# Live rows as plus and minus one, a reordered start, and loop counters raised earlier: masked self-attention on one core

## The chip, the cores and the metric

One core of one Trainium2 chip runs the whole batch as one program. The metric is device microseconds of one execution, shown as the median of the runs. Five engines work side by side: TensorE (PE, with its weight loads as PEld), VectorE (DVE), ScalarE (ACT), GpSimd (POOL) and SyncE (SP), which issues most transfers. Each engine has its own list of instructions and its own sequencer, and the lists meet only at semaphores. The times are from one fixed draw of the lengths.

## The reference

```python
batch, max_seq, n_heads, head_dim = (32, 512, 8, 64)
lengths = np.random.randint(64, max_seq, size=batch)
...
for b in range(batch):
    seq_len = lengths[b]
    qkv = np.matmul(x[b, :seq_len], w_qkv)
    q, k, v = np.split(qkv, 3, axis=-1)
    ...
    scores = scale * np.matmul(q, k.transpose(0, 2, 1))
    attn = np.exp(scores - scores_max)
    attn = attn / (np.sum(attn, axis=-1, keepdims=True) + 1e-08)
    output[b, :seq_len] = np.matmul(attn, v)...
```

Rows at and behind `seq_len` stay zero in the output. Everything is float32 in and out; the kernel multiplies in float16 with float32 sums.

## The kernel before

**Order by length.** The kernel ranks the 32 sequences by length on the chip and works them off in 16 pairs, longest first. There are twelve loops, one for each padded width N in `LOOPS` (512, 448, 384, 352 and so on by 32 down to 96). A loop runs as often as there are pairs of its width; for this draw once for 512, 448, 384, 320, 288, 256, 192, 128 and 96, three times for 352, twice for 224 and 160. A loop's body holds two positions, one for each sequence of the pair. A width has n = 4, 3, 2 or 1 tiles of 128 rows.

**Steps.** What a position does and in which order is written by hand in the table `ORDER`: S is a step of scores with its exponentials, B, Q and K are query and key projections, U, V and W values, A and Z weighted sums, E fills columns, L writes the live column, P the masks and casts, D loads, X transposes by DMA. The digits after @ are the eight PSUM banks that a step uses (512 fp32 in a partition each). A position projects the sequence behind it while it computes the weighted sums of its own. So TensorE's next group waits for a bank until VectorE or ScalarE has copied it out.

**Normalisation.** The value matmuls carry a 65th column, so that a bank holds the weighted sums of some heads and beside them the sum of each row's exponentials. VectorE then runs, for each head group, R (reciprocal of the sums into `rcp`, L1706), U (times the live rows, 1 or 0, from the live column of `v_aug` or from `queries`, L1712) and O (the bank times the broadcast `rcp` into `out_nat`, L1715). For two neighbouring banks with n = 2, or one tile, `both_normed` does this over both at once (L1671, L1680, L1693). With n = 1 `divide_live` (L1725) multiplies by the live row and `rcp` in one scalar_tensor_tensor instead of U and O.

**Waits.** Semaphores are only counted up, so a wait inside a loop compares against a register. Every engine holds `pair` and one register for each distinct amount; at the end of a loop's body it adds to each of them, and on entering a loop it works out a few more by a multiply and an add (`fixed`). TensorE's additions are rows L2115 and L2123 in its list, its branch back L2125, its entry L2088 and the loop's first compare L2102. A wait that a planner (`plan_waits`) finds to be covered by an earlier one is left out.

**The head.** Ahead of the loops the first sequence is cast to 16 bits tile by tile (L366 on VectorE, L370 on ScalarE, L371 on GpSimd), transposed on TensorE (L773) and projected: v0 to v3 (L311), then queries and keys (L300), which start with the first two quarters of the weights. The casts of the weights (L750) are shared by ScalarE and GpSimd. GpSimd also fills the ends of the `et` buffers (L590, L601). `joinPE` is the point at which TensorE waits for ScalarE's last transposed copy (L782); then come the registers, the branch and the first scores (L1269).

## Time and profile before

| what | value |
|---|---|
| runs | 329.23, 328.48, 329.05 us; median 329.05 |
| profiled execution's own time | its span, 328.5 us from the first to the last instruction; granted TensorE clock 0.994 |
| PE, ACT, DVE, POOL busy | 311.6, 262.6, 197.7, 101.9 us |
| head, until the first scores | 22.7 us |
| loops 512; 448; 384; 352 (three times) | from 22.7; 59.3; 91; 116 |
| loops 320; 288; 256; 224 (twice) | from 189; 211; 232; 246 |
| loops 192; 160 (twice); 128; 96 | from 275; 288; 310; 317 |
| end of the last division, of the store | 323.2, 328.5 us |

In the rows of the profile a start is given in us from the span's start, then the duration in us, the engine, the line, the operation, the tile written and those read, shapes, the count of merged instructions, and in brackets how long the engine stood idle before and what ended that. "issue" is time in which the engine waited for nothing that the profile shows. Where rows are grouped, the last columns are busy us, mean ns of one, and idle us before them.

### The profile page before, as it was taken

How to read it: one execution, taken by the hardware profiler on the slowest of the kernel's cores; microseconds unless marked ns; L12 is line 12 of the kernel's file. 1: busy time of each engine (PE TensorE's matmuls, PEld its weight loads, DVE VectorE, ACT ScalarE, POOL GpSimd, SP SyncE). 2: the span in 40 equal slices, each digit the busy share in tenths (PEclk: the TensorE clock that was granted, in tenths of full speed). 3: DMA queues.
4: the chain of work that ended last, by engine and by line, in shares of the span. 5: the costliest groups of instructions: out<-in, count | busy, mean ns of one | idle time of the engine just before them, and what ended most of it. 6: DMA issues, size and time to landing. Idle time of an engine off the chain costs nothing.

```text
span 328.5 us, 13310 instructions
## 1 busy us (share of the span) xinstructions
PE 311.6 (95%) x5092; PEld 202.3 (62%) x5092; DVE 197.7 (60%) x635; ACT 262.6 (80%) x413; POOL 101.9 (31%) x148
## 2 busy tenths in 40 slices
PE   6899999999999999999999999999998999999980
PEld 4444645555655556556656657667777886777860
DVE  6777567566666646456455465545575565776853
ACT  4379999897878988988978989899867779687761
POOL 6448040324030330330231243043222224435320
PEclk9999999999999999999999999999999999999997
DMA  6984749395858999696676766857459857966651
GB/s 217 382 278 80 251 140 327 76 354 153 304 52 298 224 269 258 197 268 224 233 214 224 255 194 205 211 174 242 156 131 227 183 176 164 223 206 177 193 180 66
DMA packets 69449, 68.85 MB, mean 210 GB/s; under 512 B 40720, under 2 KB 40720, under 8 KB 69392
## 3 DMA queue, kind: packets, MB, share of 16 engines
q1 hardware_dynamic: 69344, 68.12, 71.4%
q8 instruction: 33, 0.54, 0.7%
q14 instruction: 24, 0.20, 0.2%
q10 hardware_dynamic: 48, 0.00, 0.0%
HBM read 25.17 MB, written 33.55 MB: 179 GB/s over the span
## 4 chain that ended last, share of the span: by engine, by line
PE 84%; DVE 5%; DMA 3%; issue 2%; ACT 2%; SPq 1%; POOL 1%; DVEq 0%; POOLq 0%; ACTq 0%
PE banks L1323 41%; PE banks L1269 13%; PE banks L1517 12%; PE banks L300 6%; PE banks L311 6%; PE banks L1631 2%; DMA xT<-x 2%; DMA x_nat<-in_x_dram 2%; PE banks L1210 1%; PE banks L1557 1%; DVE out_nat L1715 1%; DVE rcp L1712 1%; DVE out_nat L1693 1%; SPq L328 1%; ACT et L1287 1%
## 5 line engine op out<-in xcount | busy, mean ns | idle before, releaser
L1287 ACT ACTIVATE et<-banks 128x704 f16<-128x704 f32 (+8 forms) x256 | 198.8, 825 | 27.8 <-PE banks L1269 24.7
L371 POOL TENSOR_TENSOR x<-x_nat,mask 128x512 f16<-128x512 f32 x83 | 84.2, 1041 | 184.3 <-DVE mask L1052 174.9
L1323 PE MATMUL banks<-xT,w_r 64*128 64x352 f16 (+9 forms) x1536 | 127.8, 294 | 1.8 <-DMA xT<-x 1.2
L1323 PEld LDWEIGHTS banks<-xT,w_r 64*128 64x128 f16 x1536 | 68.7, 94 | 39.0 <-PE banks L1323 8.5
L1269 PE MATMUL banks<-qz,kT 64*128 64x352 f16 (+11 forms) x624 | 77.5, 294 | 2.6 <-issue 0.7
L1715 DVE TENSOR_TENSOR out_nat<-banks,rcp 128x256 f32<-128x256 f32 (+1 forms) x110 | 53.0, 482 | 3.8
L1367 DVE CAST qz<-banks 128x448 f16<-128x448 f32 (+6 forms) x47 | 26.4, 561 | 45.2 <-PE banks L1323 44.8
L1517 PEld LDWEIGHTS banks<-v_aug,et 128*128 128x128 f16 x1240 | 41.7, 97 | 13.5 <-issue 6.8
L1517 PE MATMUL banks<-v_aug,et 128*128 128x65 f16 x1240 | 47.1, 194 | 0.0
L1323 PE MATMUL banks<-w_r,xT 64*128 64x512 f16 (+1 forms) x368 | 46.6, 372 | 0.3 <-ACT v_aug L1489 0.3
L1269 PEld LDWEIGHTS banks<-qz,kT 64*128 64x128 f16 x624 | 28.1, 93 | 25.9 <-issue 7.1
L1706 DVE RECIPROCAL rcp<-banks 128x4 f32<-128x4 f32 (+1 forms) x112 | 20.3, 181 | 20.7 <-PE banks L1517 7.3
L311 PE MATMUL banks<-w_r,xT 128*128 128x512 f16 x104 | 26.9, 381 | 0.5 <-DVE xT L782 0.5
L1386 DVE CAST v_aug<-banks 128x512 f16<-128x512 f32 x25 | 16.6, 690 | 17.9 <-PE banks L1323 17.9
L1323 PEld LDWEIGHTS banks<-w_r,xT 64*128 64x128 f16 x368 | 17.2, 94 | 14.1 <-PE banks L1323 1.0
L1367 ACT CAST kT<-banks 128x352 f16<-128x352 f32 (+6 forms) x47 | 22.5, 479 | 1.5 <-PE banks L1323 1.5
L300 PE MATMUL banks<-xT,w_r 128*128 128x160 f16 (+3 forms) x256 | 23.0, 243 | 0.5 <-DVE v_aug L1489 0.5
L1367 DVE CAST kT<-banks 128x352 f16<-128x352 f32 (+5 forms) x33 | 17.9, 552 | 7.7 <-PE banks L1323 7.6
L300 PEld LDWEIGHTS banks<-xT,w_r 128*128 128x128 f16 x256 | 16.6, 98 | 5.2 <-DMA xT<-x 0.6
L1367 ACT CAST qz<-banks 128x352 f16<-128x352 f32 (+6 forms) x33 | 15.3, 465 | 3.7 <-PE banks L1323 3.6
L1489 ACT CAST v_aug<-banks 128x512 f16<-128x512 f32 x15 | 8.8, 589 | 9.5 <-PE banks L311 9.5
L1631 PE MATMUL banks<-v_aug,et 64*128 64x65 f16 x624 | 14.2, 190 | 0.6 <-issue 0.6
(116 smaller groups left out, 193.3 us busy)
## 6 DMA issues: line engine op xcount, KB each, us to landing
x_nat<-in_x_dram SPq DMA_DIRECT2D x12, 768.0 KB, 6.4
out_dram<-out_nat SPq DMA_DIRECT2D x12, 768.0 KB, 4.0
x_nat<-in_x_dram SPq DMA_DIRECT2D x14, 512.0 KB, 4.5
out_dram<-zeros SPq DMA_DIRECT2D x12, 512.0 KB, 3.6
out_dram<-out_nat SPq DMA_DIRECT2D x12, 512.0 KB, 4.7
out_dram<-out_nat SPq DMA_DIRECT2D x4, 1024.0 KB, 7.0
x_nat<-in_x_dram SPq DMA_DIRECT2D x3, 1024.0 KB, 5.3
out_dram<-zeros SPq DMA_DIRECT2D x4, 768.0 KB, 4.7
```

Of the source, the lines that this page charges most:

```text
L300: last = nc.tensor.matmul(dst[:, 0:N], w_r[:, c, w0 : w0 + P], xT[:, c, 0:N], start=(c == 0), stop=(c == NC - 1),)
L311: last = nc.tensor.matmul(pv, xT[:, c, t * P : (t + 1) * P], w_r[:, c, 2 * D : 3 * D], start=(c == 0), stop=(c == NC - 1),)
L371: return engine.tensor_tensor(out=x16, in0=x32, in1=live.broadcast_to([P, D]), op=ALU.mult)
L1269: last = nc.tensor.matmul(psc[par][:, x * wide : x * wide + N], kT[r, i, c0 : c0 + P], qz[r, i, 0:N], start=True, stop=True,)
L1287: return nc.scalar.activation(out=et[:, :, x0:x1, 0:N], in_=got.rearrange("p j (x q) -> p j x q", q=wide)[:, :, x0:x1, 0:N], func=AF.Exp, ...
L1323: last = nc.tensor.matmul(to, lhs(rows, c), rhs(rows, c), start=(c == 0 and opens), stop=(c == NC - 1 and not opens),)
L1367: return lambda copy, bank: copy(out=buf[:, ms, 0:M], in_=bank[:, 0 : gm * M].rearrange("p (m q) -> p m q", q=M),)
L1386: return lambda copy, bank: copy(out=v_bufs[o][:, t, :, 0:HD], in_=bank.rearrange("p (h d) -> p h d", d=HD))
L1517: last = nc.tensor.matmul(pav[:, g, qt, :], e_bufs[e][:, c0 + qt * P : c0 + (qt + 1) * P], v_aug[:, kt, h, :], start=(kt == 0 and not (hal ...
L1631: last = nc.tensor.matmul(pavs[own][:, g, qt, :], e_bufs[e][rows, c0 + qt * P : c0 + (qt + 1) * P], (v_bufs[0] if ending else v_aug)[rows, ...
L1706: return nc.vector.reciprocal(out=rcp, in_=pav[:, :, :, HD])
L1715: return nc.vector.tensor_tensor(out=o_t[:, 0:n, h0 * HD : (h0 + heads) * HD].rearrange("p t (g d) -> p g t d", d=HD), in0=pav[:, :, :, 0:HD],
```

## The change

1. **Live rows.** `queries` holds 2 x alive - 1, so +1 for a live row and -1 for one behind the end. For n > 1, U comes first and multiplies the sums in PSUM by it into `rcp`; R takes the reciprocal of `rcp` in SBUF; O becomes a scalar_tensor_tensor that takes the larger of `rcp` and 0 and multiplies the bank by it, so that dead rows come out as zeros. Its patterns need the sums of a bank in the order tile, head, column. A `both_normed` over two tiles becomes two such operations. The loops of 448, 320 and 192 no longer copy the live rows into `queries` on entry (L1851); a `queries` operation is added in the head and, in loops without a half last tile, at the second position's L.
2. **The head.** The fourth tile is cast by ScalarE, its transposes stand ahead of v2, some VectorE copies change places, GpSimd's fills come behind its weight casts, two banks of the key projections are exchanged, the last key copy goes to ScalarE, and TensorE works out its first registers ahead of `joinPE`.
3. **Counters.** In the loops of `LATE`, TensorE raises `pair` and its registers ahead of its last one to three operations of the second position; these then ask for amounts that are smaller by as much. Waits for another loop's position use one of three registers set by one move at a loop's entry.
4. **The last position.** In the second position of the loop of 96, A0 over banks 3 and 4 becomes two steps of four heads.

TensorE in the head, from the first transposes to the query projections; `x_73` is the first sequence in 16 bits, L311 the value projections. Before:

```order
L773 MATMUL banks<-h_ident_117,x_73 128x128 x4
L311 MATMUL banks<-w_r,xT_75 128x512 x4
L773 MATMUL banks<-h_ident_117,x_73 128x128 x4
L311 MATMUL banks<-w_r,xT_75 128x512 x8
L773 MATMUL banks<-h_ident_117,x_73 128x128 x4
L311 MATMUL banks<-w_r,xT_75 128x512 x4
```

and with the change:

```order
L754 MATMUL banks<-h_ident_117,x_73 128x128 x4
L314 MATMUL banks<-w_r,xT_75 128x512 x4
L754 MATMUL banks<-h_ident_117,x_73 128x128 x4
L314 MATMUL banks<-w_r,xT_75 128x512 x4
L754 MATMUL banks<-h_ident_117,x_73 128x128 x4
L314 MATMUL banks<-w_r,xT_75 128x512 x8
```

The last four transposes moved ahead of v2, so that eight value matmuls follow them.

TensorE at the end of the loop of 288 and the first scores of 256 (`qz`, `kT`); ISA and REGISTER_ALU are register operations. Before:

```order
L1557 MATMUL banks<-v_aug_67,et_83 128x65
L1557 MATMUL banks<-v_aug_67,et_84 128x65
L2030 UNCONDITIONAL_BRANCH
L2115 REGISTER_ALU
L2123 ISA
L2125 COMPARE_AND_BRANCH
L2088 ISA
L2102 COMPARE_AND_BRANCH
L1269 MATMUL banks<-qz_65,kT_69 128x256 x4
```

and with the change, from a little earlier:

```order
L1284 MATMUL banks<-qz_66,kT_70 128x288 x2
L1338 MATMUL banks<-xT_75,w_r 128x256 x8
L2157 ISA
L2160 ISA
L1532 MATMUL banks<-v_aug_68,et_83 128x65 x12
L1532 MATMUL banks<-v_aug_68,et_84 128x65 x12
```

and, ten rows of L1572 further on, at the loop's end:

```order
L1572 MATMUL banks<-v_aug_67,et_83 128x65
L1572 MATMUL banks<-v_aug_67,et_84 128x65
L2090 UNCONDITIONAL_BRANCH
L2203 COMPARE_AND_BRANCH
L2179 COMPARE_AND_BRANCH
L1284 MATMUL banks<-qz_65,kT_69 128x256 x4
```

The additions stand ahead of the last value products; behind them only branches are left.

VectorE at the end of the loop of 192, the normalisations of the second position. Before:

```order
L1671 RECIPROCAL rcp_86<-banks 128x8
L1680 TENSOR_TENSOR rcp_86<-rcp_86,queries 128x8
L1693 TENSOR_TENSOR out_nat_78<-banks,rcp_86 128x4x2x64
L1706 RECIPROCAL rcp_89<-banks 128x4
L1712 TENSOR_TENSOR rcp_89<-rcp_89,queries 128x4
L1715 TENSOR_TENSOR out_nat_78<-banks,rcp_89 128x2x2x64
```

and with the change:

```order
L1708 TENSOR_TENSOR rcp_86<-banks,queries 128x8
L1699 RECIPROCAL rcp_86<-rcp_86 128x8
L1681 SCALAR_TENSOR_TENSOR out_nat_78<-rcp_86,banks 128x2x128 x2
L1747 TENSOR_TENSOR rcp_89<-banks,queries 128x4
L1743 RECIPROCAL rcp_89<-rcp_89 128x4
L1681 SCALAR_TENSOR_TENSOR out_nat_78<-rcp_89,banks 128x2x128
```

The multiply now reads PSUM, the reciprocal SBUF, and the first division is two operations.

```diff
+
+
+LATE = {320: 3, 288: 3, 256: 2, 224: 3, 192: 1, 160: 3}
...
-                after = dict(mine)
+                after = dict(clock[op.eng] if op.skip < 0 else mine)
...
-        96: "L P S0@56 K0*@7 Q0*@4 V0@0 X D A0@56 | L P S0@12 Q0*@2 K0*@1 V0*@2 X D A0@34",
+        96: "L P S0@56 K0*@7 Q0*@4 V0@0 X D A0@56 | L P S0@12 Q0*@2 K0*@1 V0*@2 X D A0@3 A4@4",
...
-        for n in range(NT, 0, -1):
-            N = min(N for N in LOOPS if tiles(N) == n)
-            for e, et in enumerate(e_bufs if n > 1 else e_bufs[0:2]):
-                op(
-                    f"et{e}.{N}",
-                    "POOL",
-                    lambda et=et, N=N: pool.memset(left_out(et, N), 0x3C003C00),
-                    ("order", f"et{e}"),
-                    (f"et{e}",),
...
             return [source.rearrange("p (j two) -> p j two", two=2)[:, :, k] for k in range(2)]
 
         cast_tile(0, 1, "ACT")
+        turn(0, 0, "bk4", "DVE")
         own = joined("own", *twos(order_i[:, 1 : B + 1]), 5, ("order",))
         later = joined("later", *twos(order_i[:, 6 : B + 6]), 5, ("order",))
         four = joined("four", own, later, 10, ("own", "later"))
-        turn(0, 0, "bk4", "DVE")
         warm("warm2", ones16, 4, 1, ())
         turn(0, 1, "bk5", "ACT")
+        read_ends("ACT", 0)
         cast_tile(0, 2, "DVE")
-        cast_tile(0, 3, "POOL")
-        step("V0", "bk0", "DVE")
+        cast_tile(0, 3, "ACT")
+        copy_v0 = step("V0", "bk0", "DVE", True)
         turn(0, 2, "bk6", "DVE")
-        read_ends("ACT", 0)
-        read_ends("ACT", 1)
-        step("V1", "bk1", "DVE")
-        copy_v2 = step("V2", "bk4", "DVE", True)
+        copy_v0()
+        copy_v1 = step("V1", "bk1", "DVE", True)
         turn(0, 3, "bk3", "DVE")
-        copy_v2()
+        copy_v1()
+        step("V2", "bk4", "DVE")
         read_ends("DVE", 0)
         shorten("wq", w_q, 0, 0, "ACT")
         shorten("wq", w_q, 0, 1, "POOL")
         read_ends("POOL", 0)
         shorten("wq", w_q, 0, 2, "ACT")
+        read_ends("ACT", 1)
         shorten("wq", w_q, 0, 3, "POOL")
         read_ends("POOL", 1)
         step("V3", "bk5", "ACT")
...
+        op(
+            "queries",
+            "DVE",
+            lambda: dve.tensor_scalar(
+                out=queries[:, 1, :], in0=alive[:, 0, :], scalar1=2.0, scalar2=-1.0, op0=ALU.mult, op1=ALU.add
+            ),
+            ("alive",),
+            ("queries0",),
...
         shorten("wk", w_k, D, 2, "POOL")
+
+        for n in range(NT, 0, -1):
+            N = min(N for N in LOOPS if tiles(N) == n)
+            for e, et in enumerate(e_bufs if n > 1 else e_bufs[0:2]):
+                op(
+                    f"et{e}.{N}",
+                    "POOL",
+                    lambda et=et, N=N: pool.memset(left_out(et, N), 0x3C003C00),
+                    ("order", f"et{e}"),
+                    (f"et{e}",),
...
-        halves("K", ("bk0", "bk1", "bk3", "bk7"), 0)
+        halves("K", ("bk7", "bk1", "bk3", "bk0"), 0)
         read_ends("PE", 2)
-        halves("K", ("bk0", "bk1"), 1, ("DVE", "ACT"))
+        halves("K", ("bk7", "bk1"), 1, ("DVE", "ACT"))
         for t, bank, eng in ((0, "bk4", "DVE"), (2, "bk6", "DVE"), (1, "bk5", "ACT"), (3, "bk2", "ACT")):
             turn(1, t, bank, eng)
-        halves("K", (None, None, "bk3", "bk7"), 1, (None, None, "DVE", "DVE"))
+        halves("K", (None, None, "bk3", "bk0"), 1, (None, None, "DVE", "ACT"))
...
                 in0=alive[:, bass.ds(at("DVE") + j, 2), 0:n],
-                scalar1=0.0,
-                scalar2=None,
-                op0=ALU.add,
+                scalar1=2.0,
+                scalar2=-1.0,
+                op0=ALU.mult,
+                op1=ALU.add,
             )
...
+        def parted(h0, sums_, r):
+
+            by = r.rearrange("p (t g) -> p t g", t=n).unsqueeze(3).broadcast_to([P, n, heads, HD])
+            return nc.vector.scalar_tensor_tensor(
+                out=o_t[:, 0:n, h0 * HD : (h0 + heads) * HD].rearrange("p t (g d) -> p t g d", d=HD),
+                in0=by,
+                scalar=0.0,
+                in1=sums_.rearrange("p (t g d) -> p t g d", t=n, d=HD + 1)[:, :, :, 0:HD],
+                op0=ALU.max,
+                op1=ALU.mult,
+            )
+
...
+            def only_live():
+                if n == 1:
+                    rows = v_aug[:, 0:n, both[0], HD]
+                    rows = rows.unsqueeze(1).broadcast_to([P, 2 * heads, n])
+                    whole_ = r.rearrange("p (g t) -> p g t", t=n)
+                    return nc.vector.tensor_tensor(out=whole_, in0=whole_, in1=rows, op=ALU.mult)
+                rows = queries[:, 1 - j, 0:n].unsqueeze(1).unsqueeze(3).broadcast_to([P, 2, n, heads])
+                return nc.vector.tensor_tensor(
+                    out=each.rearrange("p z (t g) -> p z t g", t=n),
+                    in0=total.rearrange("p z (t g) -> p z t g", t=n),
+                    in1=rows,
+                    op=ALU.mult,
                 )
...
             def divide():
+                if n > 1:
+                    for z in range(2):
+                        last = parted(both[z], sums_[:, z], each[:, z])
+                    return last
...
             held = (f"bk{k0}", f"bk{k1}")
-            whose = f"queries{j}" if half_last else f"vl{j}"
-            op(f"R{both[0]}", "DVE", reciprocal, held, (f"r{k0}",))
-            op(f"U{both[0]}", "DVE", only_live, (f"r{k0}", whose), (f"r{k0}",))
+            if n == 1:
+                op(f"R{both[0]}", "DVE", reciprocal, held, (f"r{k0}",))
+                op(f"U{both[0]}", "DVE", only_live, (f"r{k0}", f"vl{j}"), (f"r{k0}",))
+            else:
+                op(f"U{both[0]}", "DVE", only_live, (*held, f"queries{j}"), (f"r{k0}",))
+                op(f"R{both[0]}", "DVE", reciprocal, (f"r{k0}",), (f"r{k0}",))
             op(f"O{both[0]}", "DVE", divide, (*held, f"r{k0}"), tuple(f"o{j}.{h}" for h in both))
 
...
+            elif kind == "L" and not half_last and j:
+                op(
+                    "L",
+                    "DVE",
+                    lambda: (live_queries(), live(alive, 0, n))[1],
+                    (),
+                    (f"vl{o}", "queries0", "queries1"),
+                )
...
-                nc.vector.tensor_copy(out=queries[:, 1, 0:n], in_=v_bufs[0][:, 0:n, 0, HD])
...
+    tails_of = []
+    for v, N in enumerate(LOOPS):
+        mine = [k for k, op in enumerate(bodies[v][1]) if op.eng == "PE"]
+        tails_of.append(mine[len(mine) - LATE.get(N, 0) :])
+        assert not any(bodies[v][1][k].skip for k in tails_of[v])
+
+    def asked(v, j, k, op, wait):
+
+        base, amount = value_of(v, j or 0, wait)
+        if op.eng == "PE" and base in ("posin", "posold"):
+            return f"at{(v - (base == 'posold')) % 3}", amount
+        if op.eng == "PE" and j == 1 and k in tails_of[v] and base in raised and (base != "rare" or shared(LOOPS[v])):
+            return base, amount - raised[base]
+        return base, amount
...
+        def raise_all(v, e):
+            EN[e].reg_add(of(pair, e), of(pair, e), 1)
+            for (base, amount), reg in regs[e].items():
+                if base in raised and (base != "rare" or shared(LOOPS[v])):
+                    EN[e].reg_add(reg, reg, raised[base])
...
-                        for skip, ops in groupby(mine, key=lambda todo: todo[1].skip):
+                        tail = tails_of[v] if e == "PE" and j else []
+                        for skip, ops in groupby(mine[: len(mine) - len(tail)], key=lambda todo: todo[1].skip):
                             emit_all(v, j, e, skip, list(ops))
-                nc.regs_add(pair, pair, 1)
+                        if tail:
+                            raise_all(v, e)
+                            emit_all(v, j, e, 0, mine[len(mine) - len(tail) :])
                 nc.regs_add(own_pair, own_pair, 1)
-                if shared(N):
-                    for e, reg in rare_pair.items():
-                        EN[e].reg_add(reg, reg, 1)
                 for e, eng in EN.items():
-                    for (base, amount), reg in regs[e].items():
-                        if base in raised and (base != "rare" or shared(N)):
-                            eng.reg_add(reg, reg, raised[base])
+                    if e in rare_pair and shared(N):
+                        eng.reg_add(rare_pair[e], rare_pair[e], 1)
+                    if e != "PE" or not tails_of[v]:
+                        raise_all(v, e)
                 for e, eng in EN.items():
```

131 lines of the change are left out of this document (68 added, 63 removed), and 63 rows, old and new, of the table ORDER.

## The prediction

> **What bounds the kernel now.** The page comes first, then the chain that ended last, then what TensorE waited for after the part ahead of the loops.
>
> ```profile
> span 328.5 us, 13310 instructions
> PE 311.6 (95%) x5092; PEld 202.3 (62%) x5092; DVE 197.7 (60%) x635; ACT 262.6 (80%) x413; POOL 101.9 (31%) x148
> PE 84%; DVE 5%; DMA 3%; issue 2%; ACT 2%; SPq 1%; POOL 1%; DVEq 0%; POOLq 0%; ACTq 0%
> ```
>
> ```profile
> PE banks L1323 <- DMA xT<-x: 1.2, 1, 1.2
> PE banks L1269 <- issue: 0.7, 3, 0.2
> PE banks L1631 <- issue: 0.6, 1, 0.6
> ```
>
> TensorE is busy for 311.6 of 328.5 us, and the change takes no matmul away: an edit pays only where TensorE stands still. Between 23 and 323 us the page counts few microseconds of such time (the columns of the second fence: waiter, what ended the wait, us in total, times, longest). Matmuls overlap in the records, so a counted idle of 0.2 us can hide about 0.15 us more: a row with 64 columns lasts 0.19 us in the record but such matmuls start every 0.03 us. I therefore take a gap from the start of the last matmul ahead of it, and call that a bound. VectorE at 60% is free on average; its price matters only at the loop ends, where TensorE waits for the banks that VectorE empties.
>
> **The part ahead of the loops.** The chain there runs over the fourth tile of the first sequence.
>
> ```profile
> 11.53 1.04 POOL L371 TENSOR_TENSOR x<-x_nat,mask 128x512 f16<-128x512 f32 x1 [2.25 <-DMA x_nat<-in_x_dram]
> 12.62 0.40 PE L773 MATMUL banks<-h_ident,x 128*128 128x128 f16 x4 [0.27 <-POOL x L371]
> 13.01 0.62 ACT L750 CAST w_r<-w_q 128x512 f16<-128x512 f32 x1 [3.04 <-DMA w_q<-in_w_qkv_dram]
> 13.54 1.04 PE L311 MATMUL banks<-w_r,xT 128*128 128x512 f16 x4 [0.52 <-DVE xT L782]
> 14.41 6.21 PE L300 MATMUL banks<-xT,w_r 128*128 128x512 f16 x28
> 19.07 1.33 ACT L370 ACTIVATE x<-x_nat,mask 128x512 f16<-128x512 f32 x2
> 21.98 2.04 POOL L371 TENSOR_TENSOR x<-x_nat,mask 128x512 f16<-128x512 f32 x2 [4.39 <-DMA x_nat<-in_x_dram]
> 22.68 0.39 PE L1269 MATMUL banks<-qz,kT 64*128 64x512 f16 x2 [0.31 <-ACT xT L782]
> ```
>
> The tile lands just before 11.53. GpSimd casts it in 1.04 us; ScalarE takes two such casts in 1.33 us (0.67 to 0.72 each), and it was idle for 3.04 us until its first weight cast at 13.01. So the transposes at 12.62 come 0.32 us earlier. But v2, which ran before them, now stands behind them with v3: eight value matmuls at 0.22 us (four take from 13.54 to the next group's start at 14.41) follow the transposes, which start at 12.30 and take 0.23: 12.53 + 8 x 0.22 = 14.28 instead of 14.41. The gap of 0.52 us for VectorE's copy is filled by v2, and a new one opens ahead of the transposes. Net -0.14 us. GpSimd's sixteen fills move behind its weight casts, where it was idle for 4.39 us ahead of its next tile at 21.98. The first scores at 22.68 waited 0.31 us, of which the register operations now emitted ahead of that wait are, as an estimate, a quarter, 0.08. The last two K copies, both VectorE's, are now shared with ScalarE, ahead of exponentials that wait for the first scores anyway. **Head: -0.22 us** (bounds -0.45, if VectorE's shorter queue also helps, and +0.1, if GpSimd's fills slow VectorE's or ScalarE's casts beside them).
>
> **Live rows as +1 and -1.** Per head group VectorE still runs three operations, with other inputs.
>
> ```profile
> L1712 DVE TENSOR_TENSOR rcp<-rcp,queries x54: 161/164/916, 69.9 to 311.0; 128x4 f32<-128x4 f32 x38, 128x6 f32<-128x6 f32 x16
> L1715 DVE TENSOR_TENSOR out_nat<-banks,rcp 128x256 f32<-128x256 f32 x62 | 26.3, 424 | 2.1
> L1725 DVE SCALAR_TENSOR_TENSOR out_nat<-banks,real,rcp 128x256 f32<-128x256 f32 x2 | 1.0, 484 | 0.1
> L841 DVE SCALAR_TENSOR_TENSOR h_four<-h_later,h_own 128x16 f32<-128x16 f32 x1 | 0.2, 174 | 0.0
> ```
>
> The multiply that reads PSUM in place of SBUF and the reciprocal that reads SBUF in place of PSUM swap their latencies (a reciprocal of 128x4 from PSUM is 175 ns, the multiply 161): 0. For the last operation, now a scalar_tensor_tensor (STT), there is no row of its exact form. The 128x256 STT of L1725 takes 484 ns, 60 more than the tensor_tensor's 424, but it fetches its scalar from SBUF; the STT of 16 elements whose scalar is an immediate takes 174, and the multiplies of 4 to 8 elements 161 to 168, so there the form costs nothing. The new one has an immediate: I take 424, and keep +60 ns as the upper bound. The +1/-1 rows themselves cost one short tensor_scalar in the head and one at the start of a second position in the loops that had none, about 0.16 us each by the short rows above; TensorE has matmuls of that position ahead of it then, so 0, and 0.16 apiece if it ever waits there.
>
> The gain is elsewhere. One multiply with both inputs in SBUF stood in GpSimd's way:
>
> ```profile
> 23.19 0.93 DVE L1149 TENSOR_SCALAR v_aug<-alive 128x32 f16 x1
> 277.63 2.04 POOL L371 TENSOR_TENSOR x<-x_nat,mask 128x512 f16<-128x512 f32 x2 [4.10 <-DVE mask L1052]
> 278.77 0.92 DVE L1712 TENSOR_TENSOR rcp<-rcp,queries 128x4 f32<-128x4 f32 x1
> 280.57 0.45 PE L1323 MATMUL banks<-xT,w_r 64*128 64x160 f16 x8
> 281.09 0.34 PE L1269 MATMUL banks<-qz,kT 64*128 64x192 f16 x4
> ```
>
> It lasted 0.92 us instead of 0.16 and ended as GpSimd's pair of casts did (277.63 + 2.04 = 279.67). VectorE's banks came free late, and TensorE started the two groups shown late: from the start of the last matmul ahead of each, less that matmul's own spacing, 0.20 and 0.23 us. After the change the multiply has one input in SBUF. Removing the stretch is worth at most 0.43 and I take **-0.35 us**; the other stretched multiplies (in the loops of 512 and 160) have no TensorE wait behind them. The other end is 0: the reciprocal now reads SBUF, and the 0.93 us of a one-input tensor_scalar at 23.19 us, beside GpSimd's casts, show that one input can be held too. I go by the multiply, as the nearer row in form, since the tensor_scalar writes 16-bit rows and a reciprocal divides. [...]
>
> **Loop ends.** 1. *512 to 448.* VectorE's chain sets the first query copy of the new loop, and one link of it goes.
>
> ```profile
> 60.61 0.17 DVE L1851 COPY queries<-v_aug 128x4 f16<-128x4 f16 x1
> 62.27 0.26 DVE L1149 TENSOR_SCALAR v_aug<-alive 128x24 f16 x1 [1.19 <-issue]
> 62.51 0.62 DVE L1367 CAST qz<-banks 128x448 f16<-128x448 f32 x1
> 63.27 0.74 PE L1323 MATMUL banks<-xT,w_r 64*128 64x448 f16 x6 [0.17 <-DVE qz L1367]
> ```
>
> The copy of 0.17 goes, so the cast at 62.51 and TensorE's start at 63.27 come **0.16 us** earlier (0 if the 1.19 us ahead of L1149 is a fetch of code that began on its own). The copies at 320 and 192 have no TensorE wait right behind them: 0.
>
> 2. *Where TensorE's own sequencer is late.* Nothing but its register operations and branches stands between these:
>
> ```profile
> 231.81 0.36 PE L1557 MATMUL banks<-v_aug,et 64*128 64x65 f16 x12
> 232.37 0.39 PE L1269 MATMUL banks<-qz,kT 64*128 64x256 f16 x4 [0.20 <-issue]
> 275.09 0.51 PE L1269 MATMUL banks<-qz,kT 64*128 64x192 f16 x8 [0.23 <-issue]
> ```
>
> The additions now come before the last three PE operations and the entry's multiply-and-add shrinks to one move, but the branch back and the loop's first compare stay. From the last small matmul's start the gaps are about 0.36 and 0.39 us; I take two thirds off, **-0.25 us each**, and **-0.12** for the back edge of 224, where the loop goes round once. Bounds: 0, and -0.40 each.
>
> 3. *320 to 288*, and 192 to 160, are VectorE's:
>
> ```profile
> 212.60 0.56 DVE L1715 TENSOR_TENSOR out_nat<-banks,rcp 128x384 f32<-128x384 f32 x1
> 213.31 0.30 PE L1269 MATMUL banks<-qz,kT 64*128 64x288 f16 x2 [0.20 <-DVE out_nat L1715]
> 286.78 0.69 DVE L1693 TENSOR_TENSOR out_nat<-banks,rcp 128x512 f32<-128x512 f32 x1
> 287.79 0.42 DVE L1715 TENSOR_TENSOR out_nat<-banks,rcp 128x256 f32<-128x256 f32 x1
> 288.13 0.17 DVE L1706 RECIPROCAL rcp<-banks 128x4 f32<-128x4 f32 x1
> 288.62 0.38 PE L1269 MATMUL banks<-qz,kT 64*128 64x160 f16 x6 [0.36 <-DVEq L2042]
> ```
>
> At 320 to 288 an earlier TensorE only waits longer for the same bank: 0. At 192 to 160 the 128x512 operation becomes two of 128x256: a half of 0.42 holds VectorE for 0.34 (287.79 to 288.13, the last 0.08 overlap with the next operation), so two hold it for 0.68 and one of 0.69 for 0.61: **+0.07 us**. The same split falls elsewhere (two in the loop of 256, six in 224) where TensorE does not wait for VectorE.
>
> **The last position.** The result of the last sequence is now divided in two halves.
>
> ```profile
> 313.90 0.17 DVE L1706 RECIPROCAL rcp<-banks 128x4 f32<-128x4 f32 x1
> 314.71 0.48 DVE L1725 SCALAR_TENSOR_TENSOR out_nat<-banks,real,rcp 128x256 f32<-128x256 f32 x1
> 322.04 0.21 DVE L1671 RECIPROCAL rcp<-banks 128x8 f32<-128x8 f32 x1
> 322.49 0.69 DVE L1693 TENSOR_TENSOR out_nat<-banks,rcp 128x512 f32<-128x512 f32 x1
> ```
>
> VectorE reaches it at 322.04, after the other position's division and not after TensorE, so halves gain nothing by starting early. One piece took 322.04 to 323.18, 1.14 us; two halves at 313.90 took until 314.71 + 0.48 = 315.19, 1.29 us. **+0.15 us**, with nothing behind it but the store.
>
> **Sum.** -0.22 - 0.35 - 0.16 - 0.25 - 0.25 - 0.12 + 0.07 + 0.15 = -1.13 us, on the profiled execution's 328.5. The runs' median, 329.05, is 0.6 above that span; the same differences are put on the median: **327.9 us**.
>
> **Rivals.** (a) *The sequencer's time is hidden anyway* and the reciprocal is held as the multiply was: the loop ends then wait for banks, as 213.31 shows, and the terms of 0.25, 0.25, 0.12 and 0.35 fall. Left is -0.16: 328.9, no change. For it: three of the rows above name VectorE. Against it: 232.37 and 275.09 name no engine. (b) *The STT costs +60 ns*, as L1725's row has it. Where VectorE sets TensorE's start there are about three such operations at 512 to 448, two at 320 to 288, two in 192, four at 192 to 160 and two at the back edge of 160: 13 x 0.06 = +0.8, 328.7. [...] (d) *More*: code moves. The page counts one TensorE wait of 0.6 us for "issue" inside straight code (L1631, near 285 us); if the shorter code moves it beside other work, the sum is -1.13 - 0.6 - 0.2: 327.1. It can as well appear at a new place.
>
> **How the numbers follow.** Forecast 0.48, (a) 0.21, (b) 0.13, (c) 0.06, (d) 0.12. A difference of 0.2%, 0.66 us, is about what a measurement of this kernel can tell from no change: faster begins below 328.4. The forecast and (d) lie there but for a small part (some terms fall together): faster 0.58. (a), (b) and that part are no change: 0.30. (c), and a code fetch that newly falls on the path, are slower: 0.12. The range reaches from (d) with a little more, 326.7, past (a) to 329.3; (c) is left out. The forecast's own range, with its terms' bounds, is 327.1 to 328.5.
>
> **What would show it.** Right: the first scores at about 22.45 instead of 22.68; the multiply in the loop of 192 near 0.17 us and no 0.9 us reciprocal in its place; the gaps ahead of the first scores of 256 and 192 at 0.1 us or less; new 128x256 STTs at 424 ns; the last division 1.3 us long. Wrong: STTs of 480 ns or more, the same gaps under another name (a bank that VectorE still holds), or a wait named "issue" of half a microsecond at a place that had none.

## The result, and the profile after

| kernel | median, us | lowest to highest | ratio to before |
|---|---|---|---|
| before, runs beside the change | 328.48 | 327.58 to 329.23 (7 runs) | 1 |
| with the change | 330.07 | 329.38 to 331.73 (7 runs) | 1.0067 [1.0044, 1.0091] |

The change is slower, by 0.44 to 0.91%: some 2.2 us by the ratio (0.0067 x 328.48), 1.6 by the medians. The forecast was 327.9 us, in a range of 326.7 to 329.3: sign and range were both wrong.

The page of the changed kernel, its first lines and the chain that ended last:

```profile
span 329.8 us, 13311 instructions
PE 310.6 (94%) x5092; PEld 201.6 (61%) x5092; DVE 195.4 (59%) x650; ACT 264.4 (80%) x415; POOL 100.7 (31%) x147
PE 81%; DMA 6%; DVE 4%; SPq 3%; issue 2%; ACT 2%; DVEq 0%; ACTq 0%
```

TensorE's work is the same, 310.6 us of 5092 matmuls. The chain spends 81% on it instead of 84, and 6% on transfers instead of 3: the time went into new waits of TensorE. Between 23 and 325 us the view of waits names them (waiter, what ended the wait, us in total, times, longest):

```profile
PE banks L303 <- DMA xT<-x: 2.7, 2, 1.4
PE banks L1284 <- ACT v_aug L1401: 1.1, 1, 1.1
PE banks L1284 <- DVEq L2102: 0.7, 1, 0.7
```

The waits named "issue", which the forecast meant to shorten, are gone from the head of this list, as planned. Two transfers and one ScalarE cast, for which TensorE did not wait at these places before, and a longer wait for VectorE have come in their place. The head is longer too; the timeline of the changed kernel there:

```profile
3.15 2.72 PE L460 MATMUL banks<-h_ones 128*128 128x256 f16 x12 [3.15 <-POOL order_i L491]
12.98 0.62 ACT L731 CAST w_r<-w_q 128x512 f16<-128x512 f32 x1 [0.96 <-DMA w_q<-in_w_qkv_dram]
17.50 3.29 POOL L946 MEMSET et<- 128x256 int32 x14
19.14 2.61 DVE L369 TENSOR_SCALAR x<-x_nat,mask 128x512 f16<-128x512 f32 x2 [0.20 <-issue]
20.72 0.36 POOL L957 MEMSET et<- 128x128 f16 x2
23.72 0.39 PE L1284 MATMUL banks<-qz,kT 64*128 64x512 f16 x2 [0.21 <-ACT xT L763]
```

and the same two places of the kernel before:

```profile
1.93 2.74 PE L457 MATMUL banks<-h_ones 128*128 128x256 f16 x12 [1.93 <-POOL h_ones L447]
18.93 0.97 DVE L366 TENSOR_SCALAR x<-x_nat,mask 128x512 f16<-128x512 f32 x2 [0.20 <-issue]
```

The weights landed alike in the two profiles (first weight cast at 12.98 and 13.01 us), and so did the fourth tile (its cast starts at 11.30 and 11.53). The first scores start at 23.72 us instead of 22.68; the forecast was 22.45. Two rows differ. VectorE's pair of casts takes 2.61 us instead of 0.97, beside GpSimd's fills. And TensorE's first matmul starts 1.22 us later, for no work that the profile counts.

To see where the loops changed, I take the start of the first scores of each width from each trace. A stage is the time from the first scores of its width to those of the next (the last one to the end of VectorE's closing instructions, 0.03 us before the span's end and behind the store). "Six added" is the kernel before with six idle instructions on TensorE, tried below; it stands here because the profile of the kernel before has a wait of 1.2 us for a transfer inside its stage 224.

```
               head   512   448   384   352   320   288   256   224   192   160   128    96
before        22.68 36.58 33.10 25.08 72.34 21.54 21.05 14.45 28.27 12.79 22.22  7.29 11.03
six added     22.18 36.54 33.10 25.08 72.34 21.54 21.05 14.47 26.82 12.04 22.14  7.23 11.06
changed       23.72 36.56 33.02 25.05 72.30 21.50 20.88 14.43 27.93 11.66 23.96  6.85 11.87
```

From 448 to 288 the change saves what small terms were meant to save: 0.08, 0.03, 0.04, 0.04 and 0.17 us. The loss sits in the head and in stages 224 (whose end is the entry of 192), 160 and 96.

One execution is not another: over 35 runs the kernel before took 327.17 to 330.99 us. Its runs are 1.75 to 1.85 us longer than their own spans (330.99 with 329.2, for one); those of the changed kernel 1.92 to 2.73 (331.73 with 329.8, 329.43 with 326.7), so that a part of the loss lies outside the span and in no stage. By that, the profiled execution of before, with a span of 328.5, was a run of about 330.3 us, an estimate, and stood 1.2 above its median; "0.6 above that span" in the prediction compared two different quantities. The forecast difference was not touched by that. The profile of the changed kernel stands 1.7 above its median as well (331.73 against 330.07) and that of six added 1.2 below (327.42 against 328.64). The table therefore tells where a difference sits; its sum is not the loss.

### The profile page after: what moved, and what is told of

It reads as the page before. It is cut to its first block, busy times and chain, and to the rows that moved or that the text cites. A ratio compares the mean times of both kernels' runs of the same rounds, so it can differ in the third digit from the quotient of the medians.

```text
span 329.8 us, 13311 instructions
## 1 busy us (share of the span) xinstructions
PE 310.6 (94%) x5092; PEld 201.6 (61%) x5092; DVE 195.4 (59%) x650; ACT 264.4 (80%) x415; POOL 100.7 (31%) x147
## 4 chain that ended last, share of the span: by engine, by line
PE 81%; DMA 6%; DVE 4%; SPq 3%; issue 2%; ACT 2%; DVEq 0%; ACTq 0%
PE banks L1338 43%; PE banks L1284 13%; PE banks L1532 12%; PE banks L314 5%; DMA xT<-x 4%; PE banks L1646 3%; PE banks L303 3%; DMA x_nat<-in_x_dram 2%; PE banks L1225 1%; SPq L331 1%; PE banks L1572 1%; DVE x L369 1%; ACT et L1302 1%; DVE lasts L925 0%; PE banks L754 0%
## 5 line engine op out<-in xcount | busy, mean ns | idle before, releaser
L374 POOL TENSOR_TENSOR x<-x_nat,mask 128x512 f16<-128x512 f32 x82 | 83.1, 1039 | 178.8 <-DVE mask L1066 170.7
L1681 DVE SCALAR_TENSOR_TENSOR out_nat<-rcp,banks 128x256 f32<-128x256 f32 (+1 forms) x128 | 59.5, 470 | 5.0 <-DMA out_dram<-out_nat 0.7
L1747 DVE TENSOR_TENSOR rcp<-banks,queries 128x4 f32<-128x4 f32 (+1 forms) x110 | 17.5, 159 | 21.4 <-PE banks L1646 7.4
L1743 DVE RECIPROCAL rcp<-rcp 128x4 f32<-128x4 f32 (+1 forms) x110 | 20.2, 184 | 3.8
```

Of the source, the lines that this page charges most:

```text
L374: return engine.tensor_tensor(out=x16, in0=x32, in1=live.broadcast_to([P, D]), op=ALU.mult)
L1681: return nc.vector.scalar_tensor_tensor(out=o_t[:, 0:n, h0 * HD : (h0 + heads) * HD].rearrange("p t (g d) -> p t g d", d=HD), in0=by, scal ...
L1743: return nc.vector.reciprocal(out=r, in_=total if n == 1 else r)
L1747: return nc.vector.tensor_tensor(out=r.rearrange("p (t g) -> p t g", t=n), in0=total.rearrange("p (t g) -> p t g", t=n), in1=rows, op=ALU. ...
```

## The experiments

Theories after the result: (F) the fills, now beside VectorE's casts, hold them up and so the head; (C) something in the counters' part costs time at places where it adds no work; (R) the plus and minus one rows make VectorE late. The counters' part had lines that the prediction never priced. They raise the start values of a loop's semaphores to one common value, by increments at the start of TensorE's, ScalarE's and SyncE's lists:

```diff
+    by_dma = {op.name for body in bodies for ops in body for op in ops if op.dma}
+    alike = [name for name in lead if name not in by_dma | rare and lead[name]]
+    for name in alike:
+        lead[name] = max(lead[k] for k in alike)
```

With them TensorE makes nine such increments instead of one, ScalarE seven, SyncE 14 instead of 8. I call them the *alike start values*. Ratios below are to the kernel before on the same chip (medians 328.29 to 328.50).

**1. The head alone**: the kernel before with the whole of part 2 except the move of register work, fills included.

```diff
-        cast_tile(0, 3, "POOL")
+        cast_tile(0, 3, "ACT")
...
         shorten("wk", w_k, D, 2, "POOL")
+        for n in range(NT, 0, -1):
...
+                    lambda et=et, N=N: pool.memset(left_out(et, N), 0x3C003C00),
...
```

> The kernel before with the reordered head alone (fourth tile on ScalarE, its transposes ahead of v2, GpSimd's fills behind its weight casts, banks of the key projection exchanged, last key copy on ScalarE). Theory 1 (the fills hold VectorE's two casts of the second sequence): those two casts take about 2.6 us instead of 0.97, the first scores start at about 23.5 us instead of 22.68, and the time is about 0.9 us above before. Theory 2 (the head is not it; the loss is made in the small loops by transposing DMAs that land late): first scores within 0.2 us of 22.68, time within 0.4 us of before.

Measured: 329.26 us, 1.0021 [1.0003, 1.0039], slower. VectorE in this kernel:

```profile
L366 DVE TENSOR_SCALAR x<-x_nat,mask x4: 467/486/2343, 7.2 to 20.1; 128x512 f16<-128x512 f32 x4
```

(The view of one tile's instructions: ns shortest, median, longest; first and last start.) Of four casts of the same shape one took 2343 ns, 1.86 us more than the median. The first scores come at 22.65 us, as in theory 2 of the expectation, while the time, 0.7 us above before, is nearer to theory 1. What decides for the fills is this one cast, and experiments 2 and 7.

**2. The changed kernel with the fills at their old place.**

> The changed kernel with only GpSimd's fills put back at their old place. Theory 1: the two casts take 1.0 us again, the first scores start at about 22.3 us instead of 23.72, and the time is 1.4 us below the changed kernel, about 328.7 (0.2 us above before or less). Theory 2: the time stays within 0.5 us of the changed kernel's 330.07, with waits of 1 us or more for a transposing DMA in the loops of 160 and 128.

Measured: 328.89 us, 1.0013 [0.9994, 1.0032], against 1.0067 for the change; the pair of casts takes 0.88 us and the first scores start at 22.07. The stop at 192 and a wait for a transpose stay: 1.10 us from start to start at the first scores of 192, and 1.41 ahead of a group that waits for a transpose in stage 96.

**3. The rows alone**: the kernel before with part 1 only.

```diff
-                scalar1=0.0,
-                scalar2=None,
-                op0=ALU.add,
+                scalar1=2.0,
+                scalar2=-1.0,
+                op0=ALU.mult,
+                op1=ALU.add,
...
+            op(f"U{both[0]}", "DVE", only_live, (*held, f"queries{j}"), (f"r{k0}",))
+            op(f"R{both[0]}", "DVE", reciprocal, (f"r{k0}",), (f"r{k0}",))
```

> The kernel before with the live rows as +1 and -1 alone. Forecast terms: -0.35 us in the loop of 192, -0.16 at 512 to 448, +0.07 at 192 to 160, so about -0.4 us; the scalar_tensor_tensor at 420 to 424 ns for 128x256, no stretched multiply or reciprocal. If a longer VectorE chain costs at the loop ends: +0.3 us or more.

Measured: 328.41 us, 1.0000 [0.9979, 1.0021]. Theory R falls. The rows' forecast gain of some 0.4 us (0.12%) lies inside the interval, so the time alone neither shows nor excludes it.

**4. The counters alone**: the kernel before with part 3, the alike start values included.

```diff
+LATE = {320: 3, 288: 3, 256: 2, 224: 3, 192: 1, 160: 3}
...
+        lead[name] = max(lead[k] for k in alike)
...
+                        if tail:
+                            raise_all(v, e)
+                            emit_all(v, j, e, 0, mine[len(mine) - len(tail) :])
```

> The kernel before with the counters alone (raised ahead of the last value products; start values of the semaphores made alike, which adds 8 increments to the start of TensorE's list and 7 to ScalarE's). Theory 1: the first matmul at about 3.15 us instead of 1.93 but the first scores at most 0.2 us late, since the transposes wait for the sequence's first tile; loop ends -0.5 us together; time -0.3 us. A rival, that the added increments cost what they last: +0.8 to +1.2 us.

Measured: 330.27 us, 1.0051 [1.0033, 1.0069]. First matmul at 3.15 us; the gap at 192 and the waits for transposes (2.4 us, two times) are there without the head's order and without the rows. The loss, 1.7 us by the ratio, is more than either expectation had (-0.3, or +0.8 to +1.2).

**6. The counters without the alike start values** (the four lines above left out of experiment 4).

> The kernel before with the counters raised early and the new entry registers, but the start values of the semaphores left as they were, so that TensorE's list keeps its one start increment and its code stands 4 places earlier at the loop of 192 instead of 10 later. Theory P: no gap there, loop ends shorter as forecast, time 0.2 to 0.8 us below before. Theory R: time 1.2 to 1.8 us above before, as with all the counters.

Measured: 326.58 us, 0.9957 [0.9941, 0.9973]. The first matmul is back at 1.92, and the gap and the waits at 192, 160 and 96 are gone. Four lines that move no work are worth some 3 us (1.0051 against 0.9957). The gain over before, 1.4 us by the ratio, is more than the 0.2 to 0.8 expected; a part of the rest stands below, under the stretched multiply and the last position.

**7. The head alone, with the fills at their old place.**

> The kernel before with the reordered head but GpSimd's fills at their old place, ahead. Theory 1 (the fills hold VectorE's casts): first scores at about 22.3 us instead of 22.68 (22.6 to 23.6 with the fills moved), time 0.3 to 0.6 us below before and 1.0 to 1.4 us below the reordered head with them. Rival: the fills are harmless and the head's order itself loses: 0.4 us or more above before.

Measured: 327.41 us, 0.9961 [0.9938, 0.9984]; 1.85 us less by the medians than experiment 1, whose only difference is where the fills stand. Experiment 6 has the old order of the head and like landings (the fourth tile at 10.02 us, 9.84 in 7). TensorE there:

```profile
11.78 0.39 PE L777 MATMUL banks<-h_ident,x 128*128 128x128 f16 x4
13.56 6.21 PE L304 MATMUL banks<-xT,w_r 128*128 128x512 f16 x28
21.73 0.39 PE L1273 MATMUL banks<-qz,kT 64*128 64x512 f16 x2 [0.21 <-ACT xT L786]
```

and with the new order, experiment 7:

```profile
10.85 0.39 PE L773 MATMUL banks<-h_ident,x 128*128 128x128 f16 x4
12.80 6.21 PE L300 MATMUL banks<-xT,w_r 128*128 128x512 f16 x28
21.07 0.39 PE L1270 MATMUL banks<-qz,kT 64*128 64x512 f16 x2 [0.31 <-ACT xT L782]
```

Transposes come 0.93 us earlier, query projections 0.76, first scores 0.66; up to 0.18 of that is the tile's landing. The counters' part, and so experiment 6, also has the early register work: its wait ahead of the first scores is 0.21 instead of 0.31.

**5, 9 and 10. Idle increments alone.** Is it what these increments count, or that they are there? The kernel before, with 10, 3 or 6 increments of a semaphore that nobody waits for, at the start of TensorE's list:

```diff
+        padding = tc.alloc_semaphore("padding")
+        for k in range(10):
+            nc.tensor.sem_inc(padding, 1)
         pair = nc.alloc_registers("pair")
```

> The kernel before with ten increments of an unused semaphore at the start of TensorE's list and nothing else. They shift TensorE's later code by as many places as the counters edit does at the entry of the loop of 192 (10). Theory P (the counters' loss is the place of the code: where a code fetch falls): a gap of about 1 us in TensorE's sequencer behind the first compare of the loop of 192, and a time 0.8 to 1.8 us above before. Theory R (raising the counters early, or the new registers, makes the loss): no such gap, time within 0.4 us of before.

> The kernel before with three increments of an unused semaphore at the start of TensorE's list. [...] If the loss were only the increments' own time: no gap, 0.3 us above before.

> The same with six increments: the first wait stands at 7299. Theory P (place of the code): a gap of about 1 us behind the first compare of the loop of 192 and 1 to 2.8 us above before. If the loss were only the increments' own time: no gap, 0.6 us above before.

| added on TensorE | median, us | ratio | first matmul | first scores | gap after the compare at 192, at 128 |
|---|---|---|---|---|---|
| 3 | 328.07 | 0.9996 [0.9986, 1.0007] | 2.23 | 21.99 | none |
| 6 | 328.64 | 1.0008 [0.9992, 1.0025] | 2.68 | 22.18 | none |
| 10 | 331.78 | 1.0097 [1.0074, 1.0121] | 3.28 | 22.72 | 1.02, 0.66 |

Ten instructions that do nothing cost 3.2 us (0.0097 x 328.37), more than the whole change, and more than the 0.8 to 1.8 expected. Two effects are apart here. The first matmul comes about 0.14 us later per increment ((3.28 - 1.93) / 10). At first that is hidden: VectorE's first cast of a tile stands behind a chain of short operations that starts with TensorE's early matmuls (L557), and it starts 0.03 us after its tile landed with three added as with none, 0.30 with six and 0.98 with ten. The times with three and six added show no cost outside their intervals. (Single heads also differ by their landings: with none added the first scores came at 22.68 in the profile of before and at 21.73 in experiment 6.) From six to ten the time jumps by 3.1 us, of which the head has 0.54. The rest came with a gap that has nothing to do with what is counted, since nobody waits for this semaphore. TensorE at the entry of 192 with six added:

```profile
272.33 0.56 PE L1517 MATMUL banks<-v_aug,et 128*128 128x65 f16 x13
273.11 0.51 PE L1269 MATMUL banks<-qz,kT 64*128 64x192 f16 x8 [0.23 <-issue]
```

with ten added:

```profile
273.88 0.66 PE L1517 MATMUL banks<-v_aug,et 128*128 128x65 f16 x16
275.70 0.51 PE L1269 MATMUL banks<-qz,kT 64*128 64x192 f16 x8 [1.15 <-ACT v_aug L1386]
```

and in the changed kernel, with the ScalarE cast that the profile names for it:

```profile
273.65 0.66 PE L1532 MATMUL banks<-v_aug,et 128*128 128x65 f16 x16
273.76 1.08 ACT L1401 CAST v_aug<-banks 128x512 f16<-128x512 f32 x2 [0.19 <-PE banks L1338]
275.38 0.51 PE L1284 MATMUL banks<-qz,kT 64*128 64x192 f16 x8 [1.07 <-ACT v_aug L1401]
```

The cast ended at 273.76 + 1.08 = 274.84, half a microsecond before the scores: the name is the last event seen, not the cause. TensorE's sequencer records, from the same traces, say when the loop's first compare ended and when the next instruction, a wait for a semaphore that had last been raised more than 4 us before the compare ended, was taken up (elsewhere, as with six added, 0.06 us after it):

```
                 compare ends   next instruction   gap
ten added             274.46             275.48   1.02
counters alone        273.37             274.37   0.99
changed               274.01             275.17   1.16
```

Where that compare stands in TensorE's compiled list, counted from 0, sorts all fourteen kernels:

```
place of the compare at 192    kernels (experiment)          gap there
7287                           6, 8                          none
7291                           before, 1, 3, 7               none
7292                           11, 12                        none
7294, 7297                     9 (three), 10 (six added)     none
7301                           changed, 2, 4, 5              0.99 to 1.16 us
```

What they compute does not sort them: 5 is the kernel before with idle instructions, 11 the changed kernel. The same four have the second gap, 0.48 to 0.66 us at the entry of 128, and no other has. In these runs nothing but start increments moved the compare beyond 7292, and only one place above 7297 was tried.

That TensorE lacks its next instruction there is a guess, and no packet shows it. An 8 KB packet of instructions does run in the gap of the changed kernel (from 274.35 for 325 ns), but such a packet is also there without a gap (in the kernel before from 274.96 for 311 ns). The page has two queues of instructions (queue, packets, MB, share of the transfer engines):

```profile
q8 instruction: 33, 0.54, 0.7%
q14 instruction: 23, 0.19, 0.2%
```

The packet is one of q14; those of q8 have 16 KB. Whose instructions either queue carries no row names. None of q8 falls in the gap: the nearest in the changed kernel start at 256.6 and 276.05. What TensorE stops for stays open.

The packets of q8 do meet a transpose. Between 315 and 320.5 us the chain of the changed kernel reads (start, us, what):

```profile
315.27 4.18 DMA xT<-x
319.44 0.04 issue
319.49 1.02 PE banks L303 x20
```

That transpose, the last of the program, took 4.18 us from issue to landing; before, the one at the same place took 2.38. Of its 32 closing four-byte writes 30 were out by 317.31 us; then a packet of 16 KB of instructions ran from 317.45 for 0.96 us, and the last two followed at 318.39 and 318.40. In the kernel before all 32 were out by 316.54, ahead of its packet at 317.16. The same two orders part all fourteen kernels (us behind the issue of this transpose):

```
                     packet of q8   last closing write    landing
changed, 2, 4, 5     1.79 to 2.18         3.04 to 3.13    4.08 to 4.18
the ten others       2.40 or later        2.04 to 2.12    2.38 to 2.69
```

(In experiment 6 no packet of q8 came near it.) So in the four kernels with the gap this packet runs earlier behind the issue, and the last two writes come behind it; that it held them is argued from this order, and no row names it. Those two writes account for 1.1 us of the 1.8; the landing also follows the last write by 1.04 us in the four and by 0.34 in most others (0.57 at most), and that stays open. TensorE waited 1.3, 1.2, 1.1 and 0.6 us for this transpose in the change and experiments 2, 4 and 5. The other waits for transposes, 1.4 and 1.3 us in stage 160 of the change and of 4, I did not trace back; such waits also come without the gap, as the 1.2 us in stage 224 of before and 1.0 and 0.9 in experiments 1 and 9. With ten added, stage 160 is 1.4 us longer as well (23.58 against 22.14 with six): 0.60 of it is the second gap, at its end, the rest waits that I did not trace back.

**8, 11 and 12. The change mended.** Experiment 8 is the changed kernel without the alike start values and with the fills at their old place. Experiment 11 keeps the values but has SyncE make TensorE's and ScalarE's increments; experiment 12 is that with the fills back.

```diff
-                (nc.sync if owner[name] == "DVE" else EN[owner[name]]).sem_inc(
+                (nc.sync if owner[name] in ("DVE", "PE", "ACT") else EN[owner[name]]).sem_inc(
```

> The changed kernel without the alike start values and with the fills at their old place. If theories P and 1 hold and their gains add: 327.6 or less, 0.6 to 1.3 us below before; if only theory 1 holds: 0.5 to 1 us above before.

> The changed kernel with the start increments that TensorE and ScalarE make now made by SyncE; the alike start values, the registers, the fills and the rest as in the change. TensorE's first wait of the loop of 192 then stands one place later than before instead of ten. Theory P: first matmul at 1.9 us again, no gap at 192, time 1.7 to 3 us below the changed kernel (327.3 to 328.6 where before is 328.4). If the alike values themselves lose: within 0.5 us of the changed kernel, 1.5 us above before.

> The same with the fills also at their old place: the whole change with its two losing places mended. If both causes are right and add: 1.4 to 1.8 us below the run with the fills moved, first scores at about 21.1 us, 325.6 to 326.6 where before is 328.4.

| kernel | median, us | ratio | first scores |
|---|---|---|---|
| 8: no alike values, fills back | 325.81 | 0.9934 [0.9912, 0.9955] | 21.13 |
| 11: increments on SyncE | 328.26 | 1.0009 [0.9991, 1.0026] | 23.45 |
| 12: the same, fills back | 326.98 | 0.9966 [0.9952, 0.9979] | 22.00 |

Experiment 8 beats both kernels: 0.66% below before, and 4.3 us below the change (330.07 - 325.81). In 11 and 12 the start values are the same numbers as in the change, but the gap at 192 and the waits at 160 and 96 are gone: what mattered is where the increments stand. Experiment 12 missed its expectation (326.98 where 325.6 to 326.6 was said, first scores at 22.00 instead of 21.1): SyncE now makes 30 increments instead of the change's 14 and issues the load of the first tile at 5.34 us, 4.27 to 4.47 in the kernels other than 11 and 12. 11 against 12 is the fills once more, 1.28 us. The fills on GpSimd and the held cast on VectorE in experiment 11:

```profile
17.23 3.28 POOL L946 MEMSET et<- 128x256 int32 x14
18.76 2.71 DVE L369 TENSOR_SCALAR x<-x_nat,mask 128x512 f16<-128x512 f32 x2 [0.20 <-issue]
20.45 0.35 POOL L957 MEMSET et<- 128x128 f16 x2
```

Taken one by one, the first cast of the pair ends a fixed time after the last fill, in all three kernels with the fills there:

```
                last fill ends   cast starts, ns       ends   behind the fill
changed              21.080     19.142   2217        21.359   0.28
experiment 1         19.912     17.847   2343        20.190   0.28
experiment 11        20.807     18.762   2324        21.086   0.28
```

At the fills' old place the cast that runs beside them also ends 0.28 us after a fill (at 8.182 in the profile of before, a fill of 254 ns from 7.650), but there the next fill ends only 0.19 us after the cast, 533 ns long instead of 254.

## Why the prediction was wrong, step by step

The parts, each alone against before, add up to the whole within their intervals of some 0.2% each: +0.21% for the head, +0.51% for the counters, 0 for the rows, 0.72% against 0.67% measured. (The last position was not timed alone.) So two terms carry the error.

**The head (-0.22, "bounds -0.45 ... and +0.1, if GpSimd's fills slow VectorE's or ScalarE's casts beside them").** The step that failed is "GpSimd's sixteen fills move behind its weight casts, where it was idle for 4.39 us". It looked at the engine that runs the fills and not at what its neighbour runs then: VectorE's cast of the second sequence (18.93 in the profile of before). One cast is held until the last fill has ended, 2217 ns instead of 486, and the head is 1.45 to 1.65 us longer for it (experiment 1 against 7, the change against 2, 11 against 12: 22.65 and 21.07, 23.72 and 22.07, 23.45 and 22.00). In the medians it is 1.2 to 1.9 us. The bound of 0.1 was too small by more than ten times, though the profile of before had a warning that could have been quoted: of VectorE's four such casts the one at 7.55 us, beside the fills at their old place, took 636 ns, the others 485 to 487. The runs show that the cast is held, 2217 to 2343 ns in the three kernels with the fills there; why it is, and why over ten or eleven fills in a row there and over one only at the old place, they do not show.

The reorder itself was underrated. It gives some -0.6 us at the first scores, where -0.14 was said (experiment 7 against 6, one profile each: -0.66, with 0.18 for the landing and -0.10 for the early registers, which 6 alone has). The registers' -0.10 is close to the -0.08 forecast. (12.53 + 8 x 0.22 is 14.29, not 14.28; that changes nothing.) "The transposes at 12.62 come 0.32 us earlier" took the landing times of one profile; where the fourth tile lands earlier (10.02 and 9.84 us in experiments 6 and 7, 11.45 in the profile of before), transposes and projections gain 0.93 and 0.76.

**The counters (-0.25, -0.25, -0.12).** Two of the three terms were right as a mechanism and about right in size. Start to start, less a matmul's own spacing, the gap ahead of the first scores of 256 was 0.36 us, and is 0.16 in experiment 12 (0.12 in 6); that of 192 was 0.39 and is 0.11. So -0.20 and -0.28 where -0.25 each was said. The third, -0.12 for the back edge of 224, does not show: the first round of that loop takes 13.70 us in experiment 6 and 13.75 in 12, against 13.53 with six added. In the changed kernel itself the one at 256 shrank as forecast:

```profile
232.66 0.36 PE L1572 MATMUL banks<-v_aug,et 64*128 64x65 f16 x12
233.02 0.39 PE L1284 MATMUL banks<-qz,kT 64*128 64x256 f16 x4
```

233.02 names no wait any more. What failed is the list of what the part adds: the alike start values were read as bookkeeping and counted nowhere. With them TensorE and VectorE start late (first matmul at 3.15 us, and VectorE's first cast of a tile starts at 7.89 where it started at 7.13 in experiment 6), and TensorE's whole list is pushed along. The prediction had the second effect as "a code fetch that newly falls on the path", inside 12% for slower, and said of rival (d) that it "can as well appear at a new place". A stop did, 1.0 us at 192, with late transposes behind it, and the shift of TensorE's list at this place, ten instructions, was there to be read beforehand. That a stop would come of it was not: my own expectation between experiments, a gap with six added, was wrong, since 7297 has none. The cause of the stop stays open, and no run shows that it is a fetch. (In the chances, (a) and (b) alone add to 0.34, while "no change" has 0.30: the 0.06 for such a fetch was taken from them without a word.)

**Rival (d)** is neither shown nor excluded in its other sign. The "issue" wait of 0.6 us near 285 us is gone in experiment 6 and still there in 12 (0.81 from start to start near 283). But it does not go by the place of the code alone: before and experiments 1, 3 and 7, all with the compare at 7291, have 0.63, 0.08, nothing and 0.63.

**The stretched multiply and the reciprocal (-0.35).** The stretch is gone, as forecast. The multiplies and reciprocals on `rcp` in the changed kernel (count, then shortest, median and longest in ns):

```profile
L1747 DVE TENSOR_TENSOR rcp<-banks,queries x110: 151/157/166, 29.5 to 311.4; 128x4 f32<-128x4 f32 x62, 128x6 f32<-128x6 f32 x48
L1743 DVE RECIPROCAL rcp<-rcp x110: 177/179/193, 29.7 to 311.6; 128x4 f32<-128x4 f32 x62, 128x6 f32<-128x6 f32 x48
```

None of these multiplies is over 166 ns, where one took 916, and none of these reciprocals over 193. Of the two TensorE waits put down to it the one at 281.09 (0.23) is gone in experiment 3, while that at 280.57 stays as it was (0.20), also in experiment 12, where no multiply is late: it was not the multiply's. Experiments 7, 9 and 10, with the old multiply at 0.92 to 0.93 us, have the first wait (0.24 to 0.25), and experiments 4, 5 and 6, where it happens to last 0.62, 0.55 and 0.42, have not. So about -0.23 where -0.35 was said.

**The STT at 424.** The row of its form (us, mean ns, idle):

```profile
L1681 DVE SCALAR_TENSOR_TENSOR out_nat<-rcp,banks 128x256 f32<-128x256 f32 x80 | 32.9, 420 | 3.1 <-DMA out_dram<-out_nat 0.7
```

It took 420 ns where 424 was said, which ends rival (b), its +60 ns. It leaves nothing for the 0.06 of (c) either: at 128x384 the operation took 554 ns, and the tensor_tensor before 557, so that neither shape became slower.

**Rival (a)**, that the loop ends then wait for banks, was right at 192 to 160 alone, where VectorE was the bound already: TensorE now waits once for long, 0.83 us in the changed kernel (start to start, less a matmul's own spacing), where it waited 0.39 and 0.47 with six added. The +0.07 there measured +0.06, 0.67 us for two pieces against 0.61. **512 to 448** gave 0.08 of the 0.16.

**The last position (+0.15).** The two halves on VectorE:

```profile
323.77 0.18 DVE L1743 RECIPROCAL rcp<-banks 128x4 f32<-128x4 f32 x1
323.98 0.48 DVE L1755 SCALAR_TENSOR_TENSOR out_nat<-banks,real,rcp 128x256 f32<-128x256 f32 x1
324.38 0.17 DVE L1743 RECIPROCAL rcp<-banks 128x4 f32<-128x4 f32 x1
324.59 0.48 DVE L1755 SCALAR_TENSOR_TENSOR out_nat<-banks,real,rcp 128x256 f32<-128x256 f32 x1
```

From 323.77 to 324.59 + 0.48 = 325.07 is 1.30 us, with 1.29 forecast. What was missed is a gain beside it. From the first scores of 128 to the end, experiment 12 takes 17.61 us (7.00 + 10.61) and 6 takes 17.56, against 18.29 with six added; since experiment 6 has whole divisions, this is the counters' part and not the halves. About 0.24 us of it is in stage 128, at whose end the wait of TensorE for VectorE's division (0.28 us with six added) is no longer named. About 0.5 is behind the last division: from there the span ends after 4.68 to 4.83 us in the seven kernels with the counters' part and after 5.25 to 5.35 in the seven without. The store lands 2.4 to 2.6 us behind the last division in all of them, so this half microsecond is in the closing instructions. There the seven without have one packet more on q14 (24 before, 23 with the change); that GpSimd's closing instructions wait for it is a guess. No line of the change aims at this.

Experiment 12's 0.9966 is -1.1 us, and the sum of the prediction was -1.13. That is partly luck, as its parts show: the head and the end of the program gave more, the rows less, and SyncE's longer start takes some back.

## What to carry to other kernels

When work moves into a window where its engine is idle, read what the neighbouring engines run in that window, and price each of their operations as if held for the whole of it (here a cast of 486 ns took 2217). Count every instruction that a change adds at the start of a list, idle ones too: they start the engine later (here by about 0.14 us each, with ten), and together they move all the code behind them. A few idle increments put into the old kernel tell the place of code apart from what it computes, and parts timed one by one tell which term of a sum to mend: here two small moves turned +0.7% into -0.7%.

## What the runs showed of the hardware that was not expected

- Ten idle increments on TensorE cost 3.2 us, six 0.3 (inside the interval). Behind the step are a stop of 1.0 us after the compare at the entry of a loop, and one of 0.66 at another. In fourteen kernels both stops come with that compare at place 7301 of TensorE's list (four kernels) and not at 7297 or below (ten). No instruction packet explains them, and their cause is open.
- A queue of back-to-back fills on GpSimd held one VectorE cast for 2.2 to 2.3 us, until 0.28 us after the last fill had ended. The same fills at another place of the head let such a cast through 0.28 us after one of them (636 ns). Why is open.
- A 16 KB instruction packet (0.96 us in the changed kernel) ran ahead of the last two of a transpose's 32 closing writes, which came 1.0 to 1.1 us late, in all four kernels where it started within 2.2 us of the issue, and in none where it came later. The transpose landed 4.08 to 4.18 us behind its issue instead of 2.38 to 2.69.
- A semaphore increment on TensorE's own list delays the first matmul by about 0.14 us; three or six of them cost no measurable time.
- The program ends about half a microsecond earlier behind the last division in the seven kernels with the counters' part, in its closing instructions.
